# Gate rows by matrix products, branch loads in the room of h, and a new order of the hand-written head, in one hybrid layer

## The chip, the cores and the metric

The program runs on one core of a Trainium2 chip. The metric is the device time of one execution in microseconds. Before the change the median of three runs is 1047.86 us (1046.84 to 1050.57). A core has five engines with a queue of their own each: TensorE (PE, matrix products), VectorE (DVE), ScalarE (ACT), GpSimd (POOL) and SyncE (SP, which here only issues transfers). An engine takes its instructions in order; across engines they wait for each other by semaphores.

## The reference

One layer of a hybrid model is applied to 128 context tokens and 512 latent tokens (640 rows of width 1024):

```
mod = silu(cond) @ w_ada + b_ada        # shift1, scale1, gate1, shift2, scale2, gate2
h = rms_norm(x, g1) * (1 + scale1) + shift1
q, k, v, u, xr, xg, g = split(h @ w_in)                  # g: three merge gates of width 1024
merged = sigmoid(g0) * (attention(q, k, v) @ w_br_attn)
       + sigmoid(g1) * (s5(u) @ w_br_s5) + sigmoid(g2) * (rglru(xr, xg) @ w_br_lru)
x = x + gate1 * (merged @ w_out)
h = rms_norm(x, g2) * (1 + scale2) + shift2
a, b = split(h @ ffn_w_up)                               # 2816 columns each
x = x + gate2 * ((gelu(conv3(a)) * b) @ ffn_w_down)
y = rms_norm(x, g_final)
```

cond differs between the two kinds of token, so each gate is two rows of 1024 numbers: one for the context tokens, one for the latent ones.

## The kernel before

Activations lie with channels on the 128 partitions, in chunks of 128 channels (c = 0 to 7), and with the 640 tokens along the row. Each weight tile is loaded (`wr`, `wq`) and split by `split` into a rounded part `sh` (ACT, line 79) and a rest `sl` (DVE, line 82); each activation is held as two such parts as well (`hh` and `hl` for the first h, `mh` and `ml` for merged, `ath` and `atl` for the attention's output). A product is then three: high by high, high by rest, rest by high, all through `mm` (line 94), into a bank of PSUM, of which there are eight (`bank`).

Up to the attention the work of PE is mixed from a list, `fillers`, of pairs of a price and a function (`v_unit`, `gate_half`, `ada_unit`), from which `fill` puts units between the steps of the other stages. `ada_unit` makes the modulation `modt` (channels on partitions, two columns per chunk: latent and context); its `finish` multiplies by `sel`. `gate_half` makes one half of one gate chunk. For the branches 1 and 2 (S5 and RG-LRU) it multiplies the gate by the branch's product and writes the 128x640 result `tgate` to a DRAM tile `tsp`: index c holds the attention branch's gate itself, and index 16 + c the sum of the gated branches 1 and 2 (the second of them is added in DRAM, `accum_op`, line 548, on POOL's queue). Both are read back at the merge as `tg`.

**The merge** (loop over c, lines 1156 to 1169). `merge_start` loads the chunk of `w_br` and takes two banks (one for each 320 tokens). `merge_part` runs the attention branch's product over k = 0 to 3; k = 3 is the last pair of heads, and chunks 0 and 1 have their k = 0 to 2 done earlier, during the attention. Then DVE forms `acc` from `tg` and the two banks (two instructions over 320, one over 640), ACT makes `mh`, DVE makes `ml`. The `tg` buffers are two of each kind (`bufs=2`). The order of PE, DVE and ACT is here the scheduler's. Ahead of the loop stand four transfers on POOL (`gate_out`, line 1144), which write `modt`'s gate columns to DRAM (`gdr`) in the order of rows, number by number; `gate_bcast` (line 1148) later reads them back to all partitions as `gt`.

**The output product** (`out_mm`, `out_res`). For quarter qt of the columns and token tile t (128 tokens) it multiplies `mh`, `ml` (k = 0 to 7) by `w_out`, 24 products of 256 columns; `out_res` multiplies by `gt` and adds the old x (`xin`) into `x1`. Tile 4 of the last half is done in the part below.

**The head of the FFN** (the block under `manual_schedule` for DVE, ACT and PE, from line 1586). The FFN's up product is done for 22 blocks of 128 columns by seven products M1 to M7 of half the size. `prepare(n)` splits weights for the n-th product, `early` runs products on PE, `post` combines them, `norm2` takes the second norm of one token tile, `norm2_t` brings it to channels on partitions (for tile 4 by products with the diagonal `dg`), and `split_x` and `x_terms` make the parts `xbh`, `xbl`, `xth`, `xtl` of the sums of blocks of h. Here the code's order is the engines' order. After this block `early_load` (line 1321) issues the loads `wq` for two of the FFN's blocks, and the long loop over the remaining products follows.

All loads named here are issued by SP (`Q`), in program order.

Of the kernel before, what the change touches and what calls it, by code (L numbers as in the profile page):

```python
# [11 lines left out]
F32 = mybir.dt.float32  # L12
# [8 lines left out]
P = 128  # L21
# [50 lines left out]
def tile_hybrid_flow_step(ctx, tc, a, o):  # L72
# [508 lines left out]

    for hv in range(2):
        for t in range(5):
            fillers.append((2.6, lambda hv=hv, t=t: v_unit(hv, t)))
# [5 lines left out]
    fillers += adas + [(0.1, lambda: None)]  # L590
# [549 lines left out]
    gdr = pd.tile([2, 2, NK, P], F32, name="gdr")  # L1140

    def gate_out(chunk0, which):
        for q in range(2):
            G.dma_start(out=gdr[which, q].rearrange("k p -> p k"), in_=modt[:, chunk0:chunk0 + 8, q])

# [4 lines left out]
    gate_out(16, 0)  # L1150
    gate_out(40, 1)
# [3 lines left out]
    es_z, pz = pool("pz")  # L1155
    for c in range(NK):
        if c not in merging:
            merge_start(c, 0)
        merge_part(c, merging[c][2], 4)
        acc = pz.tile([P, NT], F32, tag="acc", name="acc", bufs=2)  # L1160
        tg = [pz.tile([P, NT], F32, tag=f"tg{q}", name="tg", bufs=2) for q in range(2)]
        for q in range(2):
            Q.dma_start(out=tg[q], in_=tsp[16 * q + c])
        for h in range(2):
            cs = slice(h * HT, (h + 1) * HT)
            stt(acc[:, cs], tg[0][:, cs], 1.0, merging[c][1][h][:, :HT], ADD, MUL)
        tt(acc, acc, tg[1], ADD)
        act(mh[:, c], acc, scale=0.5)
        stt(ml[:, c], acc, 0.5, f(mh[:, c]), MUL, SUB)
# [66 lines left out]
    def norm2_t(t, xn):  # L1236
# [10 lines left out]
        for z in (1, 0):  # L1247
            for k in range(4):
# [4 lines left out]
                else:  # L1253
                    ts(h32[:, kk, tk], src, sc, sh, MUL, ADD)
        n0, n1 = t * P, min((t + 1) * P, HT)
# [9 lines left out]
    def out_mm(t, b, q, w):  # L1265
        tk = slice(t * P, (t + 1) * P)
        ob = b[:, q * 256:q * 256 + 256]
        for k in range(8):
# [14 lines left out]
    for qt in range(2):  # L1283
        w = [wload(a["w_out"][qt, kk]) for kk in range(2)]
        for t in range(5):
            b = bank()
            out_mm(t, b, 0, w)
# [33 lines left out]
    def early_load(fi):  # L1321

        for z, tag in ((0, "ah"), (1, "al")):
            for k in range(2):
                t = pf.tile([P, 512], F32, tag=tag, name="wq", bufs=6)
# [68 lines left out]
    def prod_post(fi, m, o_):  # L1394
# [29 lines left out]
        elif m == "M4":  # L1424
# [5 lines left out]
            ah = pf.tile([P, NT + 1], F32R, tag="ah", name="ah", bufs=6)  # L1430
# [14 lines left out]
    def residual(bk, t, cs):  # L1445
        dt = pf.tile([P, 512], F32, tag="dt", name="dt", bufs=2)[:, 0:cs.stop - cs.start]
# [184 lines left out]
    for fi in AHEAD:  # L1631
        early_load(fi)
# [119 lines left out]
```

## Time and profile before

| | |
|---|---|
| median of 3 runs | 1047.86 us (1046.84 to 1050.57) |
| profiled execution | 1047.76 us |
| its span, first to last instruction | 1046.0 us |
| mean granted clock of PE | 0.978 |
| PE busy | 1000.0 us, 96% |
| DVE busy | 787.5 us, 75% |
| ACT busy | 468.2 us, 45% |
| POOL busy | 130.0 us, 12% |

The profiled execution lies 0.1 us from the median, so sums against its span can be read against the median as they are. Times in the rows count from the first instruction of the span. A busy PE is an upper reading: a matrix product stays "busy" for about twice as long as the distance to the next one's start, since they are pipelined, so lost time is read from the distance between starts.

### The profile page before, as it was taken

Reading aid. Unit: us, or ns where it says so; the run is one execution under the profiler, and the core shown is the slowest. Engines: PE = TensorE matmul, PEld = TensorE weight load, DVE = VectorE, ACT = ScalarE, POOL = GpSimd, SP = SyncE. Lnnn points to the kernel's source line nnn. Section 1 sums busy time; section 2 is a strip of 40 time slices with the busy share of each in tenths; the row PEclk is TensorE's granted clock in tenths of the full one; section 3 lists DMA queues with packets and bytes.
Section 4 is the critical chain, followed back from the end, with each engine's and each line's share of the span. In section 5 each row is a group of like instructions: output and inputs, shape, how many; then the busy total and the mean of one; then the engine's idle time right before and its main releaser. Section 6 shows DMA issues by size and latency. Waiting matters only on the chain.

```text
span 1046.0 us, 17692 instructions
## 1 busy us (share of the span) xinstructions
PE 1000.0 (96%) x6628; PEld 928.8 (89%) x6628; DVE 787.5 (75%) x1862; ACT 468.2 (45%) x903; POOL 130.0 (12%) x151
## 2 busy tenths in 40 slices
PE   6999899999999999999889988999999999999995
PEld 4799876889999999999889987988999899988994
DVE  6895888757756865565476589976997599966977
ACT  5256172333255654545232755532554145522544
POOL 6010730000002202022000101100110000101104
PEclk8999899999999999999889999999999999999998
DMA  9534167662433435334954032141324122321212
GB/s 365 219 115 133 37 207 255 218 214 76 139 110 130 111 84 148 102 86 117 211 181 132 21 116 87 41 141 39 93 79 133 41 81 81 103 82 58 81 61 102
DMA packets 50664, 126.32 MB, mean 121 GB/s; under 512 B 5649, under 2 KB 17809, under 8 KB 50577
## 3 DMA queue, kind: packets, MB, share of 16 engines
q1 hardware_dynamic: 48720, 120.44, 36.6%
q0 software_dynamic: 1856, 4.74, 2.1%
q8 instruction: 52, 0.85, 0.4%
q14 instruction: 36, 0.29, 0.1%
HBM read 111.10 MB, written 12.75 MB: 118 GB/s over the span
## 4 chain that ended last, share of the span: by engine, by line
PE 71%; DVE 8%; DMA 4%; ACT 2%; issue 2%; POOL 1%; SPq 0%; POOLq 0%; DVEq 0%; ACTq 0%
PE bk L94 30%; PE bM L94 23%; PE dn L94 13%; DMA tg<-tsp 2%; PE sc L94 2%; PE ptp L1061 1%; PE ob L94 1%; DVE sl L82 1%; DVE x L82 1%; ACT h L79 1%; DMA wq<-in_w_up 1%; DMA wr<-in_w_in 1%; DMA wr<-in_w_ada 1%; DVE tq L82 0%; DVE xbl L82 0%
## 5 line engine op out<-in xcount | busy, mean ns | idle before, releaser
L79 ACT ACTIVATE sh<-wr 128x512 fp32r<-128x512 f32 (+1 forms) x288 | 174.5, 618 | 230.4 <-PE dn L94 85.1
L82 DVE TENSOR_TENSOR sl<-wr,sh 128x512 fp32r<-128x512 f32 (+1 forms) x288 | 196.9, 692 | 84.9 <-ACT sh L79 84.4
L94 PE MATMUL bk<-hh,sl 128*128 128x320 f32 x608 | 189.0, 312 | 2.0 <-DVE sl L82 2.0
L94 PE MATMUL bk<-hh,sh 128*128 128x320 f32 x608 | 187.4, 316 | 1.7 <-ACT sh L79 1.4
L94 PE MATMUL bk<-hl,sh 128*128 128x320 f32 x608 | 188.9, 311 | 0.0
L94 PEld LDWEIGHTS bk<-hh,sh 128*128 128x128 f32 x608 | 114.4, 191 | 14.1 <-issue 6.2
L94 PEld LDWEIGHTS bk<-hh,sl 128*128 128x128 f32 x608 | 115.0, 189 | 4.9 <-DVE sl L82 2.6
L94 PEld LDWEIGHTS bk<-hl,sh 128*128 128x128 f32 x608 | 115.2, 189 | 2.6 <-DVE u L82 1.0
L94 PE MATMUL bM<-xth,sh 128*128 128x320 f32 x352 | 109.0, 310 | 2.2 <-ACT sh L79 2.2
L94 PE MATMUL bM<-xth,sl 128*128 128x320 f32 x352 | 108.8, 310 | 1.2 <-DVE sl L82 1.2
L94 PE MATMUL bM<-xtl,sh 128*128 128x320 f32 x352 | 108.8, 309 | 0.8 <-DVE xtl L82 0.8
L94 PE MATMUL dn<-sl,ah 128*128 128x512 f32 (+1 forms) x224 | 87.8, 392 | 0.0
L94 PE MATMUL dn<-sh,ah 128*128 128x512 f32 (+1 forms) x224 | 87.4, 390 | 0.0
L94 PE MATMUL dn<-sh,al 128*128 128x512 f32 (+1 forms) x224 | 87.3, 390 | 0.0
L94 PE MATMUL bM<-xbh,sl 128*128 128x320 f32 x264 | 81.9, 310 | 0.8 <-DVE sl L82 0.8
L94 PE MATMUL bM<-xbh,sh 128*128 128x320 f32 x264 | 82.4, 312 | 0.0
L94 PE MATMUL bM<-xbl,sh 128*128 128x320 f32 x264 | 81.9, 310 | 0.3 <-DVE xbl L82 0.3
L94 PEld LDWEIGHTS bM<-xth,sh 128*128 128x128 f32 x352 | 66.1, 188 | 3.0 <-ACT sh L79 3.0
L94 PEld LDWEIGHTS bM<-xth,sl 128*128 128x128 f32 x352 | 66.2, 188 | 1.8 <-DVE sl L82 1.8
L94 PEld LDWEIGHTS bM<-xtl,sh 128*128 128x128 f32 x352 | 66.2, 188 | 1.0 <-DVE xtl L82 1.0
L82 POOL TENSOR_TENSOR wr<-wr,s 128x512 f32<-128x512 f32 x18 | 27.5, 1526 | 314.4 <-DVE sl L82 269.8
L94 PEld LDWEIGHTS bM<-xbh,sl 128*128 128x128 f32 x264 | 49.8, 189 | 1.1 <-DVE sl L82 1.1
(400 smaller groups left out, 2206.9 us busy)
## 6 DMA issues: line engine op xcount, KB each, us to landing
wr<-in_w_up SPq DMA_DIRECT2D x40, 512.0 KB
wr<-in_w_in SPq DMA_DIRECT2D x38, 512.0 KB
wr<-in_w_ada SPq DMA_DIRECT2D x32, 512.0 KB
wr<-in_w_down SPq DMA_DIRECT2D x22, 512.0 KB
adw<-in_w_ada SPq DMA_DIRECT2D x16, 512.0 KB
tsp<-tgate SPq DMA_DIRECT2D x16, 320.0 KB
tg<-tsp SPq DMA_DIRECT2D x16, 320.0 KB
wr<-in_w_out SPq DMA_DIRECT2D x8, 512.0 KB
```

The source lines that it names most:

```text
L79: S.activation(out, in_, f, **k)
L82: e.tensor_tensor(out, x, y, op)
L94: T.matmul(out, l, r, start=start, stop=stop)
L1061: T.transpose(bt[:, c * P:(c + 1) * P], pr[:, c * P:(c + 1) * P], ident)
```

## The change

1. `gates_out` replaces `gate_out`: four products with `ident` turn the two gates' columns of `modt` (128 x 8) into 8 x 128, ACT copies them (`grow`), and SP writes them to `gdr` in runs of 128 numbers. It is the last entry of `fillers`, with a price of 0.6.
2. `tg` no longer has buffers of its own: the sixteen 128x640 loads go into `hh` and `hl`, the parts of the first h. All are issued ahead of the merge.
3. The merge's order on PE is the code's.
4. In the first quarter of the output product, tiles 0 to 2 run k = 0 to 6 first, all three, and k = 7 after.
5. In the head, `out_mm(4)`, `out_res(4)` and `norm2(4)` come right after `norm2_t(3)`'s transposes; the split of tile 3 (`norm2_s`), `sums_b(1)` and the preparations come after them; `norm2_t(4)` comes ahead of `post(0, 2)`, and after two early products instead of three; six of eight `wq` loads are issued inside the block. For that, `ah` and `dt` are buffers of the pool `pfa`, and `early_load` takes a list of halves.

```diff
+    gdr = pd.tile([2, 2, NK, P], F32, name="gdr")
+
+    def gates_out():
+
+        for which, chunk0 in ((0, 16), (1, 40)):
+            b = bank()
+            for q in range(2):
+                mm(b[0:NK, q * P:(q + 1) * P], modt[:, chunk0:chunk0 + NK, q], ident, True, True)
+            g = pv.tile([P, 256], F32, tag="mv", name="grow", bufs=2)
+            act(g[0:NK], b[0:NK, 0:256])
+            Q.dma_start(out=gdr[which].rearrange("q k p -> k q p"), in_=g[0:NK].rearrange("k (q p) -> k q p", q=2))
+
...
-    fillers += adas + [(0.1, lambda: None)]
+    fillers += adas + [(0.1, lambda: None), (0.6, gates_out)]
...
-    gdr = pd.tile([2, 2, NK, P], F32, name="gdr")
-
-    def gate_out(chunk0, which):
-        for q in range(2):
-            G.dma_start(out=gdr[which, q].rearrange("k p -> p k"), in_=modt[:, chunk0:chunk0 + 8, q])
-
     def gate_bcast(dst, which):
         for q in range(2):
             G.dma_start(out=dst[:, q], in_=gdr[which, q].rearrange("k p -> (k p)").partition_broadcast(P))
 
-    gate_out(16, 0)
-    gate_out(40, 1)
     es_g, pg = pool("pg")
     mh = pg.tile([P, NK, NT], F32R, name="mh")
     ml = pg.tile([P, NK, NT], F32R, name="ml")
     es_z, pz = pool("pz")
+    tg = [[f(x[:, c]) for x in (hh, hl)] for c in range(NK)]
     for c in range(NK):
-        if c not in merging:
-            merge_start(c, 0)
-        merge_part(c, merging[c][2], 4)
-        acc = pz.tile([P, NT], F32, tag="acc", name="acc", bufs=2)
-        tg = [pz.tile([P, NT], F32, tag=f"tg{q}", name="tg", bufs=2) for q in range(2)]
         for q in range(2):
-            Q.dma_start(out=tg[q], in_=tsp[16 * q + c])
-        for h in range(2):
-            cs = slice(h * HT, (h + 1) * HT)
-            stt(acc[:, cs], tg[0][:, cs], 1.0, merging[c][1][h][:, :HT], ADD, MUL)
-        tt(acc, acc, tg[1], ADD)
-        act(mh[:, c], acc, scale=0.5)
-        stt(ml[:, c], acc, 0.5, f(mh[:, c]), MUL, SUB)
+            Q.dma_start(out=tg[c][q], in_=tsp[16 * q + c])
+    with tc.manual_schedule(engines={mybir.EngineType.PE}):
+        for c in range(NK):
+            if c not in merging:
+                merge_start(c, 0)
+            merge_part(c, merging[c][2], 4)
+            acc = pz.tile([P, NT], F32, tag="acc", name="acc", bufs=2)
+            for h in range(2):
+                cs = slice(h * HT, (h + 1) * HT)
+                stt(acc[:, cs], tg[c][0][:, cs], 1.0, merging[c][1][h][:, :HT], ADD, MUL)
+            tt(acc, acc, tg[c][1], ADD)
+            act(mh[:, c], acc, scale=0.5)
+            stt(ml[:, c], acc, 0.5, f(mh[:, c]), MUL, SUB)
...
-    def norm2_t(t, xn):
+    def norm2_t(t, xn, then=True):
...
+        if then:
+            norm2_s(t)
+
+    def norm2_s(t):
+
...
-    def out_mm(t, b, q, w):
+    def out_mm(t, b, q, w, ks=range(NK)):
         tk = slice(t * P, (t + 1) * P)
         ob = b[:, q * 256:q * 256 + 256]
-        for k in range(8):
+        for k in ks:
...
+        if qt == 0:
+            b01 = [bank() for t in range(3)]
+            with tc.manual_schedule(engines={mybir.EngineType.PE}):
+                for ks in (range(0, NK - 1), range(NK - 1, NK)):
+                    for t in range(3):
+                        out_mm(t, b01[t], 0, w, ks)
         for t in range(5):
-            b = bank()
-            out_mm(t, b, 0, w)
+            if qt == 0 and t < 3:
+                b = b01[t]
+            else:
+                b = bank()
+                out_mm(t, b, 0, w)
...
-    def early_load(fi):
-
-        for z, tag in ((0, "ah"), (1, "al")):
+    def early_load(fi, zs):
+
+        for z, tag in ((0, "ah"), (1, "ah")) if fi == AHEAD[0] else ((0, "dt"), (1, "al")):
+            if z not in zs:
+                continue
             for k in range(2):
-                t = pf.tile([P, 512], F32, tag=tag, name="wq", bufs=6)
+                t = (pf if tag == "al" else pfa).tile([P, 512], F32, tag=tag, name="wq", bufs=2 if tag == "dt" else 6)
                 Q.dma_start(out=t, in_=a["w_up"][fi + z * NF][:, k * 512:k * 512 + 512])
...
-        norm2_t(3, xn2[3])
-        prepare(4)
-        sums_b(1)
+        norm2_t(3, xn2[3], False)
         out_mm(4, bl, 1, w_out2)
         out_res(4, bl, slice(512, 1024))
         norm2(4, lambda i: x_terms(c03, V, slice(i, i + 1)))
+        prepare(4)
+        norm2_s(3)
...
-        early(0, 1, 2)
-        post(0)
+        early_load(AHEAD[0], (0, 1))
+        early_load(AHEAD[1], (0,))
+        early(0, 1)
+        sums_b(1)
         prepare(6)
         split_x(xth[1], xtl[1], B11, c0)
+        norm2_t(4, None)
+        early(2, 3)
+        post(0, 2)
         split_x(xth[2], xtl[2], B12, c0)
-        norm2_t(4, None)
-        early(3)
-        post(2)
...
-    for fi in AHEAD:
-        early_load(fi)
+    early_load(AHEAD[1], (1,))
```

On SP, at the end of the attention, the rows before were these (`tsp` is the DRAM copy of the branches, with the buffer's number; the `w_br` rows are the merge's chunks):

```order
L1100 DMA wr<-in_w_br 128x512 x4
L112 DMA wr<-in_w_out 128x1024 x2
L1163 DMA tg<-tsp_827 128x640
L1163 DMA tg<-tsp_843 128x640
L1163 DMA tg<-tsp_828 128x640
L1163 DMA tg<-tsp_844 128x640
L1163 DMA tg<-tsp_829 128x640
L112 DMA wr<-in_w_out 128x1024
L1163 DMA tg<-tsp_845 128x640
L1163 DMA tg<-tsp_830 128x640
L1163 DMA tg<-tsp_846 128x640
```

Now they are:

```order
L1112 DMA wr<-in_w_br 128x512 x3
L1163 DMA hl<-tsp_843 128x640
L1163 DMA hh<-tsp_827 128x640
L1163 DMA hh<-tsp_828 128x640
L1163 DMA hl<-tsp_844 128x640
L1163 DMA hh<-tsp_829 128x640
...
L1163 DMA hh<-tsp_834 128x640
L1163 DMA hl<-tsp_850 128x640
L1112 DMA wr<-in_w_br 128x512
L112 DMA wr<-in_w_out 128x1024 x7
```

The sixteen reads of `tsp` are one run; the last chunk of `w_br` and seven loads of `w_out` have moved behind it, where the reads used to be spread between the loads of `w_out`.

On PE, at the same place (the attention's last products `obc`, then the merge; `ath` and `atl` are the parts of the attention's output), before:

```order
L94 MATMUL obc<-pq,vct 64x128 x2
L94 MATMUL bk<-ath,sh 128x320
L94 MATMUL bk<-atl,sh 128x320
L94 MATMUL bk<-ath,sl 128x320
L94 MATMUL bk<-ath,sh 128x320 x5
L94 MATMUL bk<-atl,sh 128x320 x3
L94 MATMUL bk<-ath,sl 128x320 x2
L94 MATMUL bk<-atl,sh 128x320
L94 MATMUL bk<-ath,sl 128x320
```

Now:

```order
L94 MATMUL obc<-pq,vct 64x128 x2
L94 MATMUL bk<-ath,sh 128x320
L94 MATMUL bk<-atl,sh 128x320
L94 MATMUL bk<-ath,sl 128x320
L94 MATMUL bk<-ath,sh 128x320
L94 MATMUL bk<-atl,sh 128x320
L94 MATMUL bk<-ath,sl 128x320
```

Before, products of several chunks that need only `ath` stood together ahead of most that need `atl` of the last pair; now the three products of a k stand in turn from the start (chunk 0, k = 3 first, which needs the last pair of heads). The number of merge products from there to the first one of the output is 156.

On DVE, in the head of the FFN, before (`x` is tile 4's `x1`; the first two `wr` rows are `sums_b(1)`; `dg` is tile 4's diagonal):

```order
L82 TENSOR_TENSOR xbl_6292<-h_6309,xbh_6289 128x4x128
L82 TENSOR_TENSOR sl<-wr,sh 128x512 x2
L82 TENSOR_TENSOR wr<-s_7038,wr 128x512
L82 TENSOR_TENSOR wr<-wr,s_7038 128x512
L82 TENSOR_TENSOR x_6296<-bk,gt_6297 128x512
L82 TENSOR_TENSOR x_6296<-x_6296,xin 128x512
L82 TENSOR_TENSOR h_6309<-h_6309 128x4x128
L88 TENSOR_SCALAR v<-ss,ss_6310 128x1
L82 TENSOR_TENSOR h_6309<-h_6309 128x4x128
L88 TENSOR_SCALAR dg<-ident,rs 128x128
```

Now:

```order
L82 TENSOR_TENSOR xbl_6285<-h_6304,xbh_6282 128x4x64
L82 TENSOR_TENSOR xbl_6287<-h_6304,xbh_6284 128x4x64
L82 TENSOR_TENSOR x_6291<-bk,gt_6292 128x512
L82 TENSOR_TENSOR x_6291<-x_6291,xin 128x512
L82 TENSOR_TENSOR h_6304<-h_6304 128x4x128
L88 TENSOR_SCALAR v<-ss,ss_6305 128x1
L82 TENSOR_TENSOR h_6304<-h_6304 128x4x128
L88 TENSOR_SCALAR dg<-ident,rs 128x128
L82 TENSOR_TENSOR sl<-wr,sh 128x512 x2
L82 TENSOR_TENSOR xbl_6287<-h_6304,xbh_6284 128x4x128
L82 TENSOR_TENSOR wr<-s_7036,wr 128x512
L82 TENSOR_TENSOR wr<-wr,s_7036 128x512
```

The addition into `x` and the row for `dg` have moved ahead of a split of `xbl`, of two splits of weights and of `sums_b(1)`. On PE the eight products `bk<-dg,x` now stand behind 24 products of the head instead of 36.

## Rows read from the trace of the kernel before

**Rows 1.** The page, the chain that ended last, by engine, tile and line.

```profile
PE bk L94 30%; PE bM L94 23%; PE dn L94 13%; DMA tg<-tsp 2%; PE sc L94 2%; PE ptp L1061 1%; PE ob L94 1%; DVE sl L82 1%; DVE x L82 1%; ACT h L79 1%; DMA wq<-in_w_up 1%; DMA wr<-in_w_in 1%; DMA wr<-in_w_ada 1%; DVE tq L82 0%; DVE xbl L82 0%
```

**Rows 2.** Windows: length, busy (x instructions) by engine, PE clock, DMA share, GB/s.

```profile
496.50:526.40 29.90, 25.93 (x158) 25.54 (x157) 15.57 (x28) 8.11 (x14) 1.13 (x2) 0.89 0.89 214
526.40:540.00 13.60, 10.08 (x53) 9.02 (x52) 9.62 (x17) 4.13 (x7) 0.00 (x0) 0.75 0.63 208
540.00:574.00 34.00, 34.00 (x291) 34.00 (x290) 21.86 (x48) 9.67 (x22) 0.57 (x1) 1.00 0.42 132
594.80:654.00 59.20, 50.88 (x319) 47.60 (x319) 53.37 (x104) 32.35 (x57) 6.68 (x7) 0.97 0.27 90
655.00:1018.00 363.00, 363.00 (x2132) 336.83 (x2131) 302.91 (x612) 154.40 (x245) 27.47 (x18) 1.00 0.26 80
```

**Rows 3.** Timeline of PE: start, length, instruction, [idle before, by whom].

```profile
484.35 0.31 PE L94 MATMUL bk<-hh,sl 128*128 128x320 f32 x1
...
505.25 0.31 PE L94 MATMUL bk<-atl,sh 128*128 128x320 f32 x1
505.40 0.31 PE L94 MATMUL bk<-ath,sl 128*128 128x320 f32 x1
509.68 0.64 PE L94 MATMUL bk<-ath,sh 128*128 128x320 f32 x1 [3.97 <-DVE acc L85]
...
526.45 0.28 PE L94 MATMUL bk<-sh,mh 128*128 128x256 f32 x1
```

**Rows 4.** Timeline of DVE, end of the attention and start of the merge.

```profile
497.66 0.28 DVE L82 TENSOR_TENSOR atl<-obc,ath 128x128 fp32r<-128x128 f32 x1
...
509.13 0.89 DVE L85 SCALAR_TENSOR_TENSOR acc<-tg,bk 128x320 f32<-128x320 f32 x2 [9.22 <-DMA tg<-tsp]
```

**Rows 5.** Timeline of POOL, which here issues transfers, same stretch.

```profile
487.14 3.91 POOL L1144 DMA_DIRECT2D gdr<-modt  x4
```

**Rows 6.** Transfers issued from 440 to 545: count, KB each, median us to landing.

```profile
tsp<-tgate POOLq DMA_DIRECT2D x4, 320.0 KB, 5.7
gt<-gdr POOLq DMA_DIRECT2D x2, 512.0 KB, 11.6
gdr<-modt POOLq DMA_DIRECT2D x4, 4.0 KB, 16.5
```

**Rows 7.** Windows of 5 us, columns as in Rows 2.

```profile
500.00:505.00 5.00, 5.00 (x36) 5.00 (x36) 0.00 (x0) 0.63 (x1) 1.13 (x2) 1.00 0.63 33
510.00:515.00 5.00, 5.00 (x20) 5.00 (x20) 4.31 (x8) 1.32 (x2) 0.00 (x0) 0.50 1.02 390
```

**Rows 8.** DVE groups from 505 to 536: count, busy, mean ns, idle before.

```profile
L85 DVE SCALAR_TENSOR_TENSOR acc<-tg,bk 128x320 f32<-128x320 f32 x16 | 7.1, 480 | 11.1 <-DMA tg<-tsp 11.1
L85 DVE SCALAR_TENSOR_TENSOR ml<-acc,mh 128x640 fp32r<-128x640 f32 x8 | 6.6, 821 | 0.2 <-ACT mh L79 0.2
L82 DVE TENSOR_TENSOR acc<-acc,tg 128x640 f32<-128x640 f32 x8 | 6.5, 819 | 1.4 <-DMA tg<-tsp 1.3
L82 DVE TENSOR_TENSOR sl<-wr,sh 128x512 fp32r<-128x512 f32 x7 | 4.8, 683 | 0.0
```

**Rows 9.** Timeline of PE at the last `finish` of the modulation.

```profile
230.07 0.95 PE L94 MATMUL bk<-sel,m 128*128 128x4 f32 x8
```

**Rows 10.** Timeline of DVE, then PE, in the head.

```profile
599.57 0.68 DVE L82 TENSOR_TENSOR x<-bk,gt 128x512 f32<-128x512 f32 x1
603.02 0.29 DVE L88 TENSOR_SCALAR dg<-ident,rs 128x128 f32<-128x128 f32 x1 [0.44 <-POOL rs L82]
...
603.36 0.82 PE L94 MATMUL bk<-dg,x 128*128 128x128 f32 x5 [3.06 <-DVE dg L88]
```

**Rows 11.** Window of the head, DVE alone, columns as in Rows 2.

```profile
594.60:650.10 55.50, 49.47 (x99) 0.97 0.28 95
```

**Rows 12.** A wait of ACT, 545 to 650 (total, times, longest).

```profile
ACT sh L79 <- DMA wq<-in_w_up: 5.5, 1, 5.5
```

**Rows 13.** Timeline of SP in the head.

```profile
623.32 3.98 SPq L1326 DMA_DIRECT2D wq<-in_w_up  x8
```

More of the change, by code (lines that the diff above doesn't have):

```diff
@@ L1429, in prod_post @@
             tt(c[:, HT + 1:], c[:, HT + 1:], u["b"], MUL)
-            ah = pf.tile([P, NT + 1], F32R, tag="ah", name="ah", bufs=6)
+            ah = pfa.tile([P, NT + 1], F32R, tag="ah", name="ah", bufs=6)
             al = pf.tile([P, NT + 1], F32R, tag="al", name="al", bufs=6)
@@ L1445, in residual @@
     def residual(bk, t, cs):
-        dt = pf.tile([P, 512], F32, tag="dt", name="dt", bufs=2)[:, 0:cs.stop - cs.start]
+        dt = pfa.tile([P, 512], F32, tag="dt", name="dt", bufs=2)[:, 0:cs.stop - cs.start]
         tt(dt, bk, gt2[:, 1 if t == 0 else 0, cs], MUL)
@@ L1470, in final @@
             cs = slice(512 * c, 512 * c + 512)
-            tag, b, p = (("ap", 2, pfa), ("ah", 6, pf), ("al", 6, pf))[(2 * t + c) % 3]
+            tag, b, p = (("ap", 2, pfa), ("ah", 6, pfa), ("al", 6, pf))[(2 * t + c) % 3]
             yo = p.tile([P, 512], F32, tag=tag, name="yo", bufs=b)
```

## The prediction

> **What bounds the kernel now.** I read the page's chain first: three quarters of the time that ends last is PE's own products, and among the few waits on it stands `DMA tg<-tsp` with 2% of the span, about 21 us of waiting and transfer, and `wq<-in_w_up` with 1% [rows 1]. So PE is the bound, and a gain can only come where PE loses time. The windows show where [rows 2]: from 655 to 1018 PE is busy for the whole 363 us at full clock, and nothing that the change moves can shorten that; from 540 to 574 it is the same. Two places are left.
>
> The first is the merge with the start of the output product. Full pace of a 320-column product is the distance of two starts, 505.40 − 505.25, which the rows round to 0.15 us and which is 0.147 over a longer run [rows 3]; of a 256-column one 34.00 / 291 = 0.117 us [rows 2]. The 156 merge products (counted in the order) need 22.9 us and took 29.9: 7.0 lost. From 526.4 to 540.0 are 53 products of 256 columns [rows 2], 6.2 us, in 13.6: 7.4 lost. Together 14.4 us. Of this 4.1 us are one wait: the last product starts at 505.40, the next at 509.68, for DVE's `acc` [rows 3], which itself waited 9.22 us for `tg<-tsp` [rows 4]. After it the granted clock was 0.50, the lower of its two levels (1.2 of 2.4 GHz), and 5 us held 20 products where full pace fits 34 [rows 7]. In 526.4 to 540.0 the clock is 0.75 [rows 2] again, behind waits for late `mh` and `ml`.
>
> Why `tg` was late: POOL issued four transfers `gdr<-modt` at 487.14 [rows 5]. They carry 4 KB each and landed 16.5 us later, where a 320 KB one (`tsp<-tgate`) took 5.7 [rows 6]. From 500 to 505, inside that time, the DMA engines were 0.63 busy and moved 33 GB/s; from 510 to 515, with reads of 320 KB, 1.02 and 390 GB/s [rows 7].
>
> The Trainium skill, page "DMA: Bandwidth & Descriptors", section "Rules for kernel authors", says that a strided last dimension is lowered to one descriptor per element. The trace agrees: 4 KB held the engines for 16.5 us.
>
> The second place is the head of the FFN: from 594.8 to 654.0 PE ran 303 products of 320 columns (44.5 us) and 16 short ones of about 0.11 (1.8 us) in 59.2 us [rows 2]: 12.9 lost. There DVE is the limit: 53.37 of 59.2 us busy [rows 2], and from 594.6 to 650.1, where its last weight part for the head ends, 49.5 busy and only 6.0 idle [rows 11].
>
> **Gates by products.** Removed: the four slow transfers, which cost PE nothing themselves. Added on PE at about 231 us: eight short product records (four products in fp32) like `sel`'s, and a wait between the first and second gate for `modt`. `sel` ran eight in 0.95 us [rows 9]; eight of 128 columns I take at 0.11 each, 0.9 us, and 0.5 us for the wait: **+1.4 us**. Below 0.9 it can't be, since PE has no idle there to hide it; 2.5 is the other end, if the second pair waits a DVE instruction of 0.68 longer [rows 8]. ACT's two copies and SP's two transfers are hidden: `gdr` is read 290 us later. The filler's price of 0.6 moves some gate halves by a unit or two; same work, so nothing, with ±1 for the range.
>
> **Branch loads in h's room.** `hh` and `hl` are last read at 484.35 [rows 3], chunk 0 some 3 us earlier, so the sixteen loads can go from about 481.2. Their 5.24 MB take 13.4 us at 390 GB/s [rows 7]; the last one also waits for the last `tsp<-tgate`, issued near 486.6, plus 5.7 [rows 6], 492.3. Queued behind them on SP are the last `w_br` chunk and seven `w_out` loads. I take T, the landing of `w_br` chunk 7, as 496 to 499. Who waits for T: ACT's split of chunk 7 stands ahead of its first `mh`, so the chain `acc`, `mh`, `ml` really runs from T on. On DVE one chunk costs (7.1 + 6.6 + 6.5) / 8 = 2.5 us and a split 0.68 [rows 8], 3.2 together, under PE's 24 × 0.147 = 3.5. Eight chunks from T = 499 end by 524.6. So `tg` is never waited for. The gate `gt` is issued only when DVE has used the last `hl` (about 523) and lands 5.7 to 11.6 us later [rows 6]; it delays DVE's `out_res`, not PE, unless it is at the far end (2 us).
>
> **Merge in the code's order.** PE loses a cover here. Behind `obc` it used to have products that need only `ath`; now chunk 0, k = 3 comes first and its second product needs `atl`, ready at 497.66 + 0.28 = 497.9 [rows 4]. So PE stands 1.3 us at 496.5, which is charged in full. From 498.0 on, 155 × 0.147: the merge ends at 520.8 instead of 526.45 [rows 3].
>
> **Last chunk held back.** Three tiles × 7 chunks × 3 products × 0.117 = 7.4 us lie between the merge's end and the first need of chunk 7, at 528.2. Chunk 7's chain from 520.8 on is 0.48 + 0.82 + about 0.8 (ACT, taken as `ml`'s) + 0.82 = 2.9 us [rows 8], 523.7, or 526.2 if a whole chunk still stands before it. It is covered. So the stretch keeps 1.3 of its 14.4 us of loss: **−13.1 us**.
>
> **Head.** Before, DVE did `x<-bk,gt` at 599.57 and `dg` at 603.02, and PE waited 3.06 us for it at 603.36 [rows 10]; PE's input for that addition was there when its output product ended at about 594.9. Now it comes first, so `dg` falls at about 598.3, when PE has just done the 24 head products that now stand before it (594.9 + 3.5 = 598.4): that gap is nearly gone. What is late next is `xbl` of tile 4 for M3: behind `dg` DVE has eight weight rows and `xbl` of tile 3 (about 5 us), `xtl`, four `h` and `xbl` (about 3 us), so 606; PE, after `dg` and 24 products, is there at 603.9 and waits some 2 us. The loads `wq`, issued at 623.32 [rows 13], go out some 25 us higher; ACT's 5.5 us wait for them [rows 12] goes, and with it DVE's behind it. But DVE's 49.5 us of work remain. I take the idle that DVE can shed: 6.0 less about 0.5 at the start, **−5.5 us**. Ends: −3 if only the `dg` gap pays, −7 if PE also runs closer behind DVE's last part. The other buffers of `ah`, `al`, `dt` change nothing: the loop behind has no lost time to lose [rows 2] and no load is issued later.
>
> Sum: 1.4 − 13.1 − 5.5 = −17.2. From the profiled 1047.76 (0.1 under the median) that is **1030.5 us**.
>
> **Rivals.**
> (A) *The head's gain vanishes*: the new M3 wait of 2 us and a lower clock after it take it back. For: the clock was at its lower level after the merge's wait [rows 7], and DVE stays the limit. Against: 6 us of DVE idle have named causes. 1047.8 + 1.4 − 13.1 = 1036.
> (B) *Part of the merge's gain is lost*. The mean rate of the merge was 214 GB/s [rows 2]; then the 5.24 MB land at 481.2 + 24.5 = 505.7, while DVE's chain has to start by 528.2 − 8 × 3.2 = 502.6: 3.1 us later, 1033.6. Or the 1.3 us wait behind `obc` brings the lower clock: 5 us of it cost 14 products, 2 us [rows 7]; with both 1036.
> (C) *Better*: the head gives 7, the obc wait hides half: 1028; with a cheaper gate unit 1026.5.
> (D) *The change doesn't do what it says*: the reads were slow for another reason than the small writes and land no earlier, so most of the 14.4 us stay; with a part of the head's gain 1043 to 1047. Against: the change of rate within 10 us, from 33 to 390 GB/s [rows 7], with the end of the small writes.
> (E) *Slower*: SP's single run of sixteen loads keeps a low rate, and `w_br` chunk 7, and with it ACT and all of the merge, waits behind them. Each us of T beyond 502.6 costs PE one. At T = 519.8 the whole gain of 17.2 is gone (5.24 MB in 38.6 us, 136 GB/s); at 525.0 it is 0.5% slower, 1053 (120 GB/s). Rates of 33 GB/s were seen only under the small writes [rows 7], which are gone.
>
> The Trainium skill (same page, section "Bandwidth") has a rule that speaks against this edit: batch transfers to 1 MiB or more for three quarters of the peak; its table gives 138 GB/s for 64 KB and 341 for 1 MB. By it, at an estimated 140 to 200 GB/s for 320 KB, T would be 507 to 519 and the kernel 1035 to 1047; that is the worse end of B and the near end of E, and it has their chances. The 390 GB/s measured with reads of 320 KB stand against it.
>
> **How the numbers follow.** Chances: as forecast (1028 to 1033) 0.55, A 0.15, B 0.13, C 0.07, D 0.07, E 0.03. The range reaches over C and A, 1025.5 to 1038, and leaves out D, E and the worse part of B. 0.5% is 5.2 us, about what a measurement of this kernel can tell: faster than 1042.6 is all but D and E and a little, 0.91; D gives most of 0.06 for the same; E 0.03 slower.
>
> **What would show it.** No `gdr<-modt` on POOL; no wait of `acc` for a load; PE without the gaps at 505 and 528 and at clock 1.00 there; a new gap of some 1.3 us behind `obc`; the first output product 5.7 us earlier, the stretch's end 13 us earlier. In the head: the `dg` gap near zero, a wait of about 2 us ahead of M3, `wq` no longer waited for, DVE without idle time. At 231 us, 1.4 us more. I am wrong if T lies beyond 502.6, if the head's DVE work still ends as late behind its start as now (55.5 us), or if the gate unit holds PE longer than 2.5 us.

## The result, and the profile after

| | median, us | ratio to the kernel before, 95% interval |
|---|---|---|
| first comparison | 1038.05 (before 1049.21) | 0.9895 [0.9867, 0.9924] |
| the same kernel again, five executions | 1040.14 (before 1048.01) | 0.9931 [0.9903, 0.9959] |

The change makes the kernel faster, by 0.7 to 1.1%, but 1038.05 lies just above the range of 1025.5 to 1038.0, 1040.14 more clearly so, and the forecast of 1030.5 was 8 to 10 us too low. One of the first four executions, the profiled one, had PE near half clock from end to end (1620 us); it counts in the 1038.05 (the other three alone have a median of 1037.96, at the very edge of the range) but not in the ratio, and the profile shown here is that of the second comparison, 1041.47 us with a span of 1039.7.

The page's chain by engine, tile and line, which answers to [rows 1]:

```profile
PE bk L94 36%; PE bM L94 23%; PE dn L94 13%; DMA wr<-in_w_in 2%; DVE tb L82 1%; DVE sl L82 1%; PE sc L94 1%; PE ptp L1073 1%; PE ob L94 1%; DVE x L82 1%; PE gp L94 1%; ACT h L79 1%; DMA kc<-in_kct 1%; DVE vt L82 1%; SPq L1016 0%
```

`tg<-tsp` (2%) and `wq<-in_w_up` (1%) are gone from it; `ptp` has stayed, and a part of it will matter. To see where the time went I cut both spans at the same instructions of PE: the last `sel`, the first score product (`sc`), the attention's last product (`obc`), the first product that reads `mh`, the last one, and the first down product (`dn`). Windows (columns as in [rows 2]) of the kernel before:

```profile
230.76:324.37 93.61, 93.61 (x647) 93.60 (x646) 62.14 (x119) 41.56 (x86) 7.72 (x10) 1.00 0.37 112
324.37:496.32 171.95, 171.26 (x1294) 165.19 (x1293) 112.04 (x319) 93.00 (x221) 23.75 (x30) 1.00 0.43 109
496.32:526.45 30.13, 26.16 (x163) 25.63 (x160) 15.62 (x28) 8.24 (x14) 1.13 (x2) 0.89 0.89 212
526.45:594.75 68.30, 64.33 (x514) 63.10 (x513) 43.04 (x85) 28.86 (x71) 3.79 (x7) 0.95 0.36 115
594.75:683.85 89.10, 80.78 (x523) 77.48 (x522) 83.22 (x171) 49.03 (x85) 9.98 (x9) 0.98 0.26 82
```

And of the changed kernel:

```profile
233.18:328.38 95.20, 94.83 (x654) 94.25 (x654) 60.88 (x117) 41.77 (x87) 7.73 (x10) 1.00 0.34 107
328.38:507.07 178.69, 172.94 (x1295) 165.87 (x1293) 111.87 (x320) 93.90 (x223) 19.90 (x26) 0.99 0.45 123
507.07:531.57 24.50, 23.51 (x162) 23.05 (x159) 21.11 (x38) 9.97 (x16) 0.00 (x0) 1.00 0.52 180
531.57:593.10 61.53, 60.70 (x514) 60.32 (x512) 37.11 (x77) 27.30 (x68) 4.90 (x9) 1.00 0.37 121
593.10:678.20 85.10, 79.58 (x524) 75.98 (x522) 82.98 (x171) 48.97 (x85) 10.00 (x9) 1.00 0.25 79
```

Read the second number, the length. The third and fourth rows, merge and output product, went from 98.4 to 86.0 us, with the clock at 1.00 and DMA share down from 0.89 to 0.52 in the merge. The fifth, the head, went from 89.1 to 85.1. The second, the attention, went the other way: from 171.95 to 178.69, with the same products. The whole, from start to PE's last product:

| stage | before | changed | difference | forecast |
|---|---|---|---|---|
| start to last `sel` | 230.8 | 233.2 | +2.4 | 0 |
| to the first score product (gate unit) | 93.6 | 95.2 | +1.6 | +1.4 |
| attention | 172.0 | 178.7 | **+6.7** | 0 ±1 |
| merge and output product | 98.4 | 86.0 | −12.4 | −13.1 |
| head and the loop behind it | 439.5 | 434.8 | −4.7 | −5.5 |
| sum | 1034.3 | 1027.9 | −6.4 | −17.2 |

The first row is taken for scatter: PE's instructions there, and their order, are the same in all kernels here, and their profiles give 228.5 to 233.8 for it (e10 alone 239.5, for a reason given there).

The waits of PE from 300 to 510 in the changed kernel (total, times, longest; `prc` are probabilities, `kk` and `kf` parts of the keys):

```profile
PE ptp L1073 <- DVE prc L88: 3.6, 1, 3.6
PE sc L94 <- DVE kk L85: 1.1, 1, 1.1
PE bk L997 <- ACT kf L79: 1.1, 1, 1.1
PE bk L94 <- ACT ath L79: 0.6, 1, 0.6
PE bk L94 <- DVE atl L82: 0.3, 1, 0.3
```

The last two are the forecast new wait behind `obc`, 0.9 us of idle time where 1.3 were forecast. Of the first three only the last has a counterpart before, where PE waits in the attention for nothing else:

```profile
PE bk L985 <- ACT kf L79: 0.7, 1, 0.7
```

The timeline of PE (start, length) around the largest, for `prc`, changed kernel:

```profile
460.82 0.31 PE L94 MATMUL bk<-uh,sl 128*128 128x320 f32 x1
...
462.74 0.60 PE L1073 MATMUL ptp<-ident,pr 128*128 128x128 f32 x4
...
463.54 0.28 PE L94 MATMUL sc<-kk,ql 128*128 128x256 f32 x1
467.39 0.52 PE L1073 MATMUL ptp<-ident,prc 128*128 128x128 f32 x2 [3.57 <-DVE prc L88]
```

Behind the last product of a unit (460.82) there are only transposes of `pr` and short score work: PE stands from 463.8 to 467.4 until DVE has `prc`, the context tokens' probabilities of this pair of heads. The kernel before, at the same point:

```profile
457.22 0.31 PE L94 MATMUL bk<-hh,sh 128*128 128x320 f32 x1
...
461.47 0.31 PE L94 MATMUL bk<-uh,sl 128*128 128x320 f32 x1
461.62 0.60 PE L1061 MATMUL ptp<-ident,pr 128*128 128x128 f32 x4
...
462.54 0.38 PE L1061 MATMUL ptp<-ident,prc 128*128 128x128 f32 x2
```

There a gate half and a branch product (`bk<-hh,sh` to `bk<-uh,sl`, 457.22 to 461.47) stood in front of the same transposes, and nothing waited. The changed kernel has spent this unit of work earlier: in its trace two such units stand back to back on PE from 436.1 to 445.0.

### The profile page after: what moved, and what is told of

The parts are those of the page before. It is cut to its first block, busy times and chain, and to the rows that moved or that the text cites. A ratio compares the mean times of both kernels' runs of the same rounds, so it can differ in the third digit from the quotient of the medians.

```text
span 1618.5 us, 17713 instructions
## 1 busy us (share of the span) xinstructions
PE 1598.1 (99%) x6636; PEld 1293.6 (80%) x6636; DVE 795.9 (49%) x1862; ACT 477.1 (29%) x905; POOL 122.4 (8%) x147
## 4 chain that ended last, share of the span: by engine, by line
PE 99%; DVE 0%; DMA 0%; ACT 0%; issue 0%; SPq 0%; POOL 0%; POOLq 0%; ACTq 0%
PE bk L94 48%; PE bM L94 27%; PE dn L94 16%; PE ob L94 2%; PE ptp L1073 2%; PE sc L94 2%; PE gp L94 1%; PE bk L428 1%; PE vtp L366 0%; PE bk L1252 0%; DMA pk<-in_pk 0%; DVE prc L88 0%; PE scc L94 0%; ACT sq L79 0%; PE obc L94 0%
## 5 line engine op out<-in xcount | busy, mean ns | idle before, releaser
L94 PE MATMUL bk<-hl,sh 128*128 128x320 f32 x608 | 263.1, 433 | 0.0
L94 PE MATMUL bk<-hh,sl 128*128 128x320 f32 x608 | 262.3, 432 | 0.0
L94 PE MATMUL bk<-hh,sh 128*128 128x320 f32 x608 | 257.8, 434 | 0.0
L94 PE MATMUL bM<-xtl,sh 128*128 128x320 f32 x352 | 152.2, 432 | 0.0
L94 PE MATMUL bM<-xth,sh 128*128 128x320 f32 x352 | 151.8, 432 | 0.0
L94 PE MATMUL bM<-xth,sl 128*128 128x320 f32 x352 | 151.8, 432 | 0.0
L94 PE MATMUL dn<-sh,al 128*128 128x512 f32 (+1 forms) x224 | 127.6, 570 | 0.0
L94 PE MATMUL dn<-sh,ah 128*128 128x512 f32 (+1 forms) x224 | 127.3, 568 | 0.0
L94 PEld LDWEIGHTS dn<-sl,ah 128*128 128x128 f32 x224 | 49.3, 220 | 36.1 <-issue 21.6
L94 PEld LDWEIGHTS dn<-sh,ah 128*128 128x128 f32 x224 | 49.2, 220 | 35.3 <-issue 19.9
```

The source lines that it names most:

```text
L94: T.matmul(out, l, r, start=start, stop=stop)
```

## The experiments

Every kernel was timed in three rounds beside the kernel before. Lengths are from one profile each, cut as above; "rest" is head and loop. e1 to e4, e5 to e8, e9 to e12 and e13 to e15 were timed on four different chips, on which the kernel before had medians from 1046.55 to 1050.12, so between these groups the ratios and the lengths say more than the medians. The lengths repeat well: the merge takes 24.5 or 23.3 us in every kernel without the small writes beside it.

| run | start to `sel` | to `sc` | attention | merge | output | rest | median, us | ratio, 95% |
|---|---|---|---|---|---|---|---|---|
| before | 230.8 | 93.6 | 172.0 | 30.1 | 68.3 | 439.5 | 1047.86 | |
| changed (e1) | 233.2 | 95.2 | 178.7 | 24.5 | 61.5 | 434.8 | 1040.14 | 0.9931 [0.9903, 0.9959] |
| e2, old head | 229.8 | 95.2 | 179.3 | 24.5 | 61.4 | 439.4 | 1044.05 | 0.9978 [0.9955, 1.0001] |
| e3, old gates | 229.1 | 93.6 | 171.5 | 31.7 | 69.2 | 434.8 | 1045.22 | 0.9977 [0.9952, 1.0001] |
| e4, nothing held back | 231.4 | 95.2 | 178.1 | 24.5 | 63.5 | 434.8 | 1041.59 | 0.9940 [0.9915, 0.9966] |
| e5, price 0 | 228.6 | 95.2 | 172.9 | 24.5 | 61.8 | 435.4 | 1032.53 | 0.9870 [0.9836, 0.9904] |
| e6, before + price | 228.5 | 93.6 | 176.9 | 30.9 | 67.7 | 439.7 | 1052.99 | 1.0064 [1.0041, 1.0086] |
| e7, before + gates | 233.0 | 95.2 | 171.4 | 23.3 | 61.7 | 438.7 | 1035.73 | 0.9894 [0.9866, 0.9921] |
| e8, e5 + scheduler | 233.8 | 95.2 | 172.7 | 23.3 | 62.9 | 434.8 | 1032.68 | 0.9870 [0.9839, 0.9901] |
| e9, e7 + head | 231.0 | 95.2 | 171.6 | 23.3 | 61.5 | 435.4 | 1031.53 | 0.9823 [0.9791, 0.9854] |
| e10, early writes | 239.5 | 93.6 | 171.1 | 23.3 | 61.9 | 434.8 | 1039.15 | 0.9896 [0.9865, 0.9927] |
| e11, e9, loads late | 229.5 | 95.2 | 171.3 | 23.3 | 61.7 | 436.5 | 1033.66 | 0.9862 [0.9820, 0.9904] |
| e12, e9, old order | 232.5 | 95.2 | 172.4 | 23.3 | 61.6 | 436.5 | 1033.81 | 0.9844 [0.9812, 0.9877] |
| e13, `prc` on ACT | 228.6 | 95.4 | 173.5 | 24.5 | 62.8 | 434.8 | 1033.25 | 0.9855 [0.9831, 0.9878] |
| e14, `cb` on DVE | 230.9 | 95.2 | 171.6 | 24.5 | 62.1 | 434.8 | 1032.98 | 0.9851 [0.9823, 0.9879] |
| e15, e9 + `prc` on ACT | 231.0 | 95.2 | 171.2 | 23.3 | 62.3 | 435.4 | 1030.86 | 0.9821 [0.9786, 0.9855] |

**e1, the changed kernel again, and e2, e3, e4: one part undone each.**

> The changed kernel again, unaltered, for a profile at full clock (the first one had TensorE held at about half clock throughout). Theory 1: the merge gave its 13 us and the head of the FFN almost nothing, so PE still loses 11 to 13 us between the end of the output product and the end of the head, and 1 to 2 us in the merge. Theory 2: the merge kept 4 to 8 us of its loss (late loads, or a wait behind the attention's last products followed by the lower clock), and the head gave its 5 us. Time 1038 either way.

The profile is the one above. Both theories fell: merge and head came as forecast.

e2 is the changed kernel with every edit to the head and to its buffers undone:

```diff
-        norm2_t(3, xn2[3], False)
+        norm2_t(3, xn2[3])
+        prepare(4)
+        sums_b(1)
...
-        early_load(AHEAD[0], (0, 1))
-        early_load(AHEAD[1], (0,))
```

> The changed kernel with the head of the FFN, its early loads and its buffers as before. Theory 1 (head gives nothing): 1038, no difference that can be measured. Theory 2 (head gives 5.5, the merge less than forecast): 1043 to 1044.

1044.05, and the rest takes 439.4 instead of 434.8: the head does give its gain, 4.6 us.

e3 takes back the gate unit:

```diff
-    fillers += adas + [(0.1, lambda: None), (0.6, gates_out)]
+    fillers += adas + [(0.1, lambda: None)]
...
+    gate_out(16, 0)
+    gate_out(40, 1)
```

> The changed kernel with the gates written element by element from POOL at the end of the attention, as before, and without the unit at 231 us. If the small writes were what held the reads back, the reads that stand behind 487 us slow down again and the gain shrinks by 3 to 10 us: 1041 to 1048. If the reads are early enough to be ahead of the small writes, or the writes were not the cause, it is 1.4 us faster than the changed kernel: 1036 to 1037.

The merge and the output product lose all of their gain (31.7 + 69.2), though the reads of `tsp` now go out from 479 on. The SP timeline of e3:

```profile
479.32 0.33 SPq L1159 DMA_DIRECT2D hl<-tsp  x1
...
495.48 0.32 SPq L1159 DMA_DIRECT2D hl<-tsp  x1
495.89 0.60 SPq L1100 DMA_DIRECT2D wr<-in_w_br  x1
```

its ACT's waits from 476 to 526:

```profile
ACT sh L79 <- DMA wr<-in_w_br: 16.1, 1, 16.1
```

and its transfers in the same stretch (KB each, median us to landing):

```profile
gdr<-modt POOLq DMA_DIRECT2D x4, 4.0 KB, 17.9
```

The last read and the last `w_br` chunk, issued at 495.5 and 495.9, meet the small writes, and ACT stands 16.1 us for that chunk. That is the mechanism of rival E, with the small writes as its cause. And the attention is back at 171.5.

e4 leaves out the block that runs k = 0 to 6 of three tiles first:

```diff
-        if qt == 0:
-            b01 = [bank() for t in range(3)]
...
-                        out_mm(t, b01[t], 0, w, ks)
```

> The changed kernel without the held-back last chunk: three tiles of the output product run k = 0 to 7 in turn. By the forecast PE then waits for the last chunk's parts at 523.3 until 523.7 to 526.2: 0.5 to 3 us slower, 1038.5 to 1041. If the DVE chain runs late (theory 2), more: 4 to 7 us slower, up to 1045.

The output product takes 63.5 instead of 61.5: 2.0 us, in the forecast's span.

**e5 and e6: the price alone.**

```diff
-    fillers += adas + [(0.1, lambda: None), (0.6, gates_out)]
+    fillers += adas + [(0.1, lambda: None), (0.0, gates_out)]
```

> The changed kernel with one number changed: the price of the gate unit in the list of fillers is 0 instead of 0.6. PE's order in the attention is then again that of the kernel before. Theory P (the price moves gate halves of other units together, so that the end of a tile's attention has no work to cover its softmax): the stretch from the first score product to the attention's last one falls from 178.7 us to 172, and the kernel from 1040 to 1034. Theory Q (the unit's own products, copies and transfers cost it): the stretch stays at 178 to 179, the kernel at 1040.

One number: the attention falls to 172.9, the kernel to 1032.53. PE's waits in the attention (columns as above) no longer show `prc`:

```profile
PE sc L94 <- DVE kk L85: 1.3, 1, 1.3
PE bk L997 <- ACT kf L79: 0.3, 1, 0.3
```

e6 is the kernel before with an entry that does nothing:

```diff
-    fillers += adas + [(0.1, lambda: None)]
+    fillers += adas + [(0.1, lambda: None), (0.6, lambda: None)]
```

> The kernel before with one entry more in the list of fillers, of price 0.6, that does nothing. No instruction is added. Theory P: the same stretch rises from 172 to 178 to 179 us and the kernel from 1048 to 1054, slower than before. Theory Q: no difference, 1048.

1052.99, slower than before, with the attention at 176.9 and the same wait:

```profile
PE ptp L1061 <- DVE prc L88: 3.6, 1, 3.6
```

So the loss is the price's, and not the unit's: theory P held, in both directions.

**e7 to e9: which part carries the merge.** e7 is the kernel before with `gates_out` as in the change, but at price 0, and without `gate_out`; nothing else.

> The kernel before with the gates written by products (price 0) and nothing else of the change: reads into their two pairs of buffers, the scheduler's order, the old head. If the small writes alone made the reads late, the merge and the start of the output product lose 1 to 4 us instead of 14.5, and the time is 1036 to 1039. If two pairs of buffers and the late issue of the reads (from 494) matter as well, 5 to 9 us stay lost and it is 1041 to 1045.

Merge and output product take 23.3 + 61.7 = 85.0 us, 1 us less than with the whole change. Waits of PE, then of DVE, in that stretch:

```profile
PE bk L94 <- ACT mh L79: 0.4, 1, 0.4
DVE acc L82 <- DMA tg<-tsp: 0.8, 2, 0.6
```

The reads into two pairs of buffers, issued from 498 on and so as late as before, are never late by more than 0.6 us. The small writes alone were the cause: without them the loss goes (e7), with them it comes back in spite of the other edits (e3).

e8 is e5 without the line `with tc.manual_schedule(engines={mybir.EngineType.PE}):` around the merge.

> As the run with price 0, but with the merge's order on PE left to the scheduler as before. If the code's order is worth nothing by itself: within 1 us of the run with price 0, 1033 to 1035, and the wait of about 1 us behind the attention's last products is smaller. If the scheduler's order (products that need only the high part first, of several chunks) finishes chunk 0 late and holds the DVE chain: 2 to 5 us slower, 1036 to 1039.

The merge is 1.2 us shorter (no wait behind `obc`), the output product 1.1 longer: nothing in all.

e9 is e7 with the changed kernel's head.

> The kernel before with the gates by products (price 0) and the new head, without the reads in h's room, without the code's order in the merge and without the held-back chunk. If these three give nothing once the small writes are gone: the merge and the output product take the 85 us of the run with the gates alone, the head 4 to 5 us less than there, 1031. If they matter: slower than the run with price 0, 1033 to 1036.

1031.53: the reads in h's room, the merge's order and the held-back chunk give nothing once the small writes are gone.

**e10: the small writes, only earlier.** e10 is e9 with the gates written number by number again, from the place of `gates_out` in the list.

```diff
-            b = bank()
...
+            for q in range(2):
+                G.dma_start(out=gdr[which, q].rearrange("k p -> p k"), in_=modt[:, chunk0:chunk0 + NK, q])
```

> As the run before it in this list, but the gates are written number by number from POOL, as in the kernel before, only at the place in the list of fillers where the products stood (about 231 us), so without products and copies. If the small writes harm only the loads that stand behind them in their 17 us: PE saves the 1.6 us of the unit, and loses what weight loads come late at 231; with no load late 1029.5, with the loads of two units late 1033 to 1036. If the products are needed to have no harm anywhere: 1036 or more.

1039.15, as expected for the case that the products are needed. The edit does not put all four writes at one place. The order of POOL is here the scheduler's, and the two writes of the first gate need no more than that gate's columns of `modt`; they went out at 158.3, the other two at 240.8. The timeline of POOL, and the transfers issued from 150 to 200:

```profile
158.30 2.03 POOL L588 DMA_DIRECT2D gdr<-modt  x2 [18.10 <-DVE modt L82]
240.80 1.76 POOL L588 DMA_DIRECT2D gdr<-modt  x2 [80.47 <-DVE modt L82]
...
gdr<-modt POOLq DMA_DIRECT2D x2, 4.0 KB, 15.2
```

Windows (columns as in [rows 2]) under the first pair and under the second, then the timeline of PE and its waits from 139 to 232:

```profile
165.00:170.00 5.00, 4.21 (x26) 3.82 (x26) 5.00 (x10) 1.91 (x4) 0.00 (x0) 1.00 0.79 44
240.00:245.00 5.00, 5.00 (x36) 5.00 (x36) 3.70 (x10) 3.53 (x9) 1.76 (x2) 1.00 0.38 46
...
173.89 1.92 PE L94 MATMUL bk<-wr,cpad 128*32 128x512 f32 x4 [4.68 <-DMA wr<-in_w_ada]
...
PE bk L94 <- DMA wr<-in_w_ada: 7.3, 2, 4.7
```

From 165 to 170 DMA moved 44 GB/s, where e9 has 237. PE waited for `w_ada` until 173.9, about when the first pair landed (158.3 + 15.2), and the granted clock was 0.50 from 173.8 to 184.0. The stretch to `sel` is 8.5 us longer than in e9; the medians differ by 7.6. Under the second pair PE was busy all the time, no engine waited for a load, and the stages behind cost PE 1.6 us less, as expected. So here too the writes held back the loads that stood among them, and another place in the list is no cure by itself.

**e11 and e12: the head's two halves.** e11 is e9 with all `wq` loads behind the block; e12 is e9 with the old order and the early loads.

```diff
# e11
-        early_load(AHEAD[0], (0, 1))
-        early_load(AHEAD[1], (0,))
...
+    early_load(AHEAD[0], (0, 1))
-    early_load(AHEAD[1], (1,))
+    early_load(AHEAD[1], (0, 1))
```

> As the combined run, with the head's new order but the eight wq loads issued behind the block, as before. If the order carries the head's gain (the 3 us wait for dg): the head takes 86 to 87 us, 1 to 1.5 us slower than the combined run. If the loads carry it (ACT's 5.5 us wait for wq): 88 us, 3 us slower.

> As the combined run, with six wq loads issued inside the block but the head's order on PE, DVE and ACT as before. If the order carries the gain: the head takes 87.5 to 88.5 us, 2.5 to 3.5 us slower than the combined run. If the loads carry it: 86 us, 1 us slower.

The rest takes 438.7 with neither (e7), 436.5 with either, 435.4 with both: 2.2 each, 3.3 together. Cut at the first `dn`, the parts come apart. The head takes 88.3 us with neither, 85.7 with the order alone, 86.8 with the loads alone and 85.7 with both: there the order carries the gain, and the loads add nothing to it. The loop behind takes 350.4, 350.8, 349.7 and 349.7: the loads' share, 0.7 to 1.1 us, lies there. These are differences of single profiles; the medians, 1031.5 to 1033.8 for e9, e11 and e12, lie too close to tell them apart.

**e13 to e15: why the bare step costs 3.6 us.** In the changed kernel, DVE and POOL at that place:

```profile
463.77 3.77 DVE L88 TENSOR_SCALAR prc<-prc,stc 128x128 f32<-128x128 f32 x2
462.81 4.43 POOL L82 TENSOR_TENSOR cb<-bias,mask 128x256 f32<-128x256 f32 x6
```

and all eight `prc` instructions of DVE (min, median and max in ns):

```profile
L88 DVE TENSOR_SCALAR prc<-prc,stc x8: 275/286/3569, 367.6 to 499.1; 128x128 f32<-128x128 f32 x8
```

The one that took 3569 ns ended with POOL's run of `cb` additions (462.81 + 4.43 = 467.24). The kernel before has this long `prc` as well, under the gate unit's cover. e13 moves `prc` to ACT in the changed kernel, e14 moves `cb` to DVE:

```diff
# e13
-                ts(pr[:, hd * P:(hd + 1) * P], pr[:, hd * P:(hd + 1) * P], st[:, 4 + hd:5 + hd], None, MUL, ALU.bypass)
+                act(pr[:, hd * P:(hd + 1) * P], pr[:, hd * P:(hd + 1) * P], scale=st[:, 4 + hd:5 + hd])
# e14
-                tt(cb[:, hd, y], bias[:, 16 - 8 * y:272 - 8 * y], mask[:, y], ADD, G)
+                tt(cb[:, hd, y], bias[:, 16 - 8 * y:272 - 8 * y], mask[:, y], ADD)
```

> The changed kernel (price 0.6) with the two instructions that normalise the context's probabilities (prc, 128x128) on ACT instead of DVE. In the changed kernel the first of them took DVE 3.57 us, against 0.28 elsewhere, while POOL ran its six additions for cb, and PE waited 3.6 us for it. Theory R (POOL's run holds DVE, and the missing cover lays it bare): the wait at the end of the third tile falls to at most 1 us, the stretch from the first score product to the attention's last one from 178.7 to 176, the kernel from 1040 to 1037. Theory S (the uncovered chain itself takes that long, whichever engine does it): no difference.

PE's wait for `prc` in e13:

```profile
PE ptp L1073 <- ACT prc L79: 0.3, 1, 0.3
```

> The changed kernel (price 0.6) with POOL's six additions of cb on DVE. Theory R: prc takes 0.28 us in all tiles; the six additions take DVE some 2 to 2.5 us, which stand ahead of prc or behind it, so the wait falls to 0 to 2 us: 1037 to 1039. Theory S: no difference or slower, 1040 to 1042.

`prc` on DVE in e14:

```profile
L88 DVE TENSOR_SCALAR prc<-prc,stc x8: 277/281/289, 363.9 to 489.8; 128x128 f32<-128x128 f32 x8
```

and PE's wait for it:

```profile
PE ptp L1073 <- DVE prc L88: 0.4, 1, 0.4
```

Theory R held: with either engine out of the other's way the wait falls from 3.6 to 0.3 or 0.4 us, and the attention to 173.5 and 171.6, at the price of 0.6 and with its order of fillers. The kernels are some 4 us below what was expected. Part of it is the lower clock behind the wait, which went with it and which the expectation had left out (it is read below); the stretch to `sel` was also 2 to 5 us shorter in these profiles, and in e14 the two short waits for `kk` and `kf` are gone.

> The combined run (gates by products at price 0, new head, nothing else) with prc on ACT. PE did not wait for prc there, so both theories say no difference: 1031 to 1032.

1030.86 against 1031.53: no difference, as both said. e9 and e15 are the fastest versions found, 1.8% under the kernel before.

## Why the prediction was wrong

**The step that failed** stands in "Gates by products": "The filler's price of 0.6 moves some gate halves by a unit or two; same work, so nothing, with ±1 for the range." The stretch grew by 6.7 us. The work is the same, but its place is its worth: the gate halves are what PE does while DVE and ACT make probabilities. One unit fewer in front of the third tile's last transposes laid a DVE chain bare that POOL's additions had stretched, and PE stood for 3.6 us. Behind that the granted clock fell to the lower of its two levels for 3.4 us (window of PE: length, busy, clock, DMA share, GB/s):

```profile
468.50:471.90 3.40, 3.40 (x29) 0.50 0.22 78
```

Half of 3.4 us, 1.7, is my estimate of what that cost. Together 5.3 us are the price's. The rest are the waits for `kk` and `kf`, 2.2 us against 0.7 before, which kernels without the price have as well (1.6 in e5). e6, which has the price and no wait for `kk`, lost 4.9 us, also with 3.4 us of the lower clock behind the wait; e5, e13 and e14 have none of it in the attention. e5 and e6 show the price as the cause, e13 and e14 the stretched instruction as what it laid bare. The prediction saw that units would move, and did not ask which wait each had covered.

**The gate unit itself**: forecast +1.4, measured 1.6. The timeline of PE has the wait for `modt` in it:

```profile
233.37 0.60 PE L94 MATMUL bk<-ident,modt 128*8 128x128 f32 x4
234.34 0.60 PE L94 MATMUL bk<-ident,modt 128*8 128x128 f32 x4 [0.37 <-DVE modt L82]
```

**The merge and the output product**: −12.4 against −13.1; the new wait behind `obc` is there, the wait for the reads and the lower clock are gone. But the part that I credited was wrong in its division: e7 gives 13.4 with the gates alone. "So `tg` is never waited for" all but holds without the room of h (0.8 us in two waits). The 16.5 us of the small writes are a time to landing, with the DMA engines 0.63 busy [rows 7]; that one descriptor goes out per element, no row here shows. By the Trainium skill's rule against transfers under 1 MiB (page "DMA: Bandwidth & Descriptors", section "Bandwidth") this stretch should have suffered, as the prediction took it; no read of 320 KB was waited for in e1, so the trace does not bear it out here.

**The head**: −4.7 against −5.5, of which 4.0 lie ahead of the first `dn` and 0.7 in the loop, where nothing was forecast. The part that was mis-sized is the idle time of DVE. Up to the same weight part as in [rows 11], again 99 instructions (window of DVE: length, busy, clock, DMA share, GB/s)

```profile
592.95:644.76 51.81, 49.54 (x99) 1.00 0.28 93
```

its work is the 49.5 us that the prediction held fixed, but it shed 3.7 us of idle time and not 5.5: 2.3 are left. The timeline of DVE, then PE:

```profile
597.11 0.29 DVE L88 TENSOR_SCALAR dg<-ident,rs 128x128 f32<-128x128 f32 x1 [0.44 <-POOL rs L82]
...
597.45 2.05 PE L94 MATMUL bk<-dg,x 128*128 128x128 f32 x16 [0.56 <-DVE dg L88]
...
603.91 0.41 PE L94 MATMUL bM<-xbh,sh 128*128 128x320 f32 x1 [0.89 <-ACT xbh L79]
...
605.01 0.41 PE L94 MATMUL bM<-xbl,sh 128*128 128x320 f32 x1 [0.69 <-DVE xbl L82]
```

`dg` at 597.1 leaves 0.56 us of the 3.06 us gap [rows 10], and the waits at M3 (603.91 and 605.01) sum to 1.6 us, where some 2 were forecast. The loads, from 580.7 on (first and last issue, in us), are waited for no more:

```profile
L1348 SPq DMA_DIRECT2D wq<-in_w_up x8: 327/425/434, 580.7 to 620.7; - x8
```

In some profiles (e5, e9, e11, e15) this new wait brings the lower clock, as rival A had it. In e9 (window, columns as in [rows 2]):

```profile
594.00:599.00 5.00, 4.53 (x20) 4.54 (x21) 3.96 (x7) 2.65 (x5) 0.00 (x0) 0.66 0.00 2
```

the granted clock falls to 0.66 behind it; in e1 it stayed at 1.00, and the head is 0.6 us shorter.

**The range** had ±1 for the fillers, and rivals for every part but this one. With e5 the sum would have held: 1032.5 against 1030.5 (or 1034.1 by e5's ratio, from 1047.76). One reading of the chain was loose without effect: its PE entries sum to 70%, not to three quarters [rows 1].

## What to carry to other kernels

A number that only orders work is an edit to every place where that work covers a wait: lay the rows of before and after side by side at each wait that is hidden now, and price what lies bare if its cover goes. When several edits aim at one stall, find the one that removes its cause; here a four-byte scatter in a queue, and three other edits were worth nothing beside it, while another place for the scatter only moved the harm. Time the parts apart before keeping them together.

## What was not expected of the hardware

A DVE instruction over 128x128 fp32 took 3.57 us instead of 0.28 while POOL ran six additions back to back, and ended when POOL's run ended, not when the addition in progress did (six in 4.43 us). A reciprocal and a reduction that DVE did under the same run (463.36 and 463.45) took 0.17 and 0.40 us, as elsewhere. And it is not always so: in the first tile of the same trace the two `prc` came under six such additions and took 1.26 us together (POOL, then DVE):

```profile
365.04 4.38 POOL L82 TENSOR_TENSOR cb<-bias,mask 128x256 f32<-128x256 f32 x6 [0.27 <-DVE stc L1039]
...
367.55 1.26 DVE L88 TENSOR_SCALAR prc<-prc,stc 128x128 f32<-128x128 f32 x2
```

What tells the two cases apart is not settled. POOL's records differ: 1.01 to 1.06 us for each addition in the long case, 0.72 to 0.91 in the short one, with starts about 0.7 us apart in both.

The Trainium skill, page "SBUF — State Buffer", section "SBUF: two separate sides", says that VectorE and GpSimd share a pair of ports by an exclusive lock held for one instruction, which VectorE needs in a two-port mode or with two inputs from SBUF. The trace agrees that one of them waits, and in the first tile with the length; in the long case it differs: the wait went over the four or five additions that were left. That the port is what holds it is argued from the page; the runs show only that either engine's absence removes it.

The four-byte writes landed 15.2 to 17.9 us after their issue where loads were due, and those came late with them: ACT waited 16.1 us for a chunk of `w_br` in e3, PE 7.3 us for `w_ada` in e10. The second pair in e10, with no load due, landed after 10.3 us and cost PE nothing.
